# Two hyena projections on the un-normed input, scaled by 1/rms afterwards

## The chip, the cores and the metric

One core of a Trainium2 chip runs one launch of the kernel. The metric is the device time of that launch in microseconds (us). The kernel before takes 2434.83 us (median of 3 runs, 2433.78 to 2437.77).

## The reference, cut to what matters

The model is an encoder of four layers on one sequence of 512 tokens with 1024 channels, all in float32. Each layer adds a mixer and then a SwiGLU feed-forward block (2816 wide) to x. The mixers are hyena, window attention, pooling, hyena. Only the two hyena mixers (layers 0 and 3) are touched.

```
def rmsnorm(x, g):
    y = x * rsqrt(mean(x * x, axis=-1, keepdims=True) + EPS)
    return y * g

def hyena_mixer(xn, ...):                  # xn = rmsnorm(x, norm_mix[i])
    p = xn @ w_in + b_in                   # 1024 -> 3 * 1024
    pp = pad(p, one token on either side)
    p = conv_b + sum(pp[:, j:j + L] * conv_w[j] for j in range(3))
    x1, x2, v = split(p, 3, axis=-1)
    kf = rfft(hyena_filters(L, ...))       # an MLP with sine units on positions, independent of x
    z = v
    for o, gate in enumerate((x1, x2)):
        z = gate * (long_conv(z, kf[:, o]) + fbias[o] * z)
    return z @ w_out + b_out
```

The norm divides every token's channels by one number, so the product of the un-normed x * g with `w_in`, scaled by 1/rms of each token, is the same sum. The bias `b_in` comes after that scale.

## The kernel before

x stands channel by token: 8 tiles of 128 channels by 512 tokens. Every float32 value that goes into a matmul is split into a rounded part and a rest (`hi`, `lo` of weights; `ghs`, `gls` of the normed input), and a product is three passes on TensorE: hi with hi, lo with hi, hi with lo (`mm3`, L206 to L208). A weight tile (512 KB, `raw`) is loaded on SyncE's queue, cast on ScalarE (`hi`, L191) and its rest taken on VectorE (`lo`, L192), 4 times 2 instructions of 128x512 for each pair of tiles.

A hyena mixer cuts each of the three projections (part 0 and 1 the gates, part 2 the value v) into four groups of 256 channels. A job (part, group) is 2 output tiles x 8 input tiles x 3 passes = 48 passes of 128x512. Its sums stand in two `mm` banks of PSUM. `in_proj` reads them with three ScalarE activations (which add the bias and the padding, L604 to L606), runs a 3-tap convolution (one activation L609 and two VectorE instructions L611), and turns the result on TensorE (L629). The groups' long convolutions follow (`conv_in` L657, `conv_out` L703 and L706), then the output projection, whose sums VectorE adds into x (L724).

Ahead of the first projection stands the norm: squares on ScalarE (L224), their sum over tiles on VectorE (`ssq`, L225), a matmul with a matrix of means (L228), a small chain for the reciprocal root (L234 to L240), a matmul that spreads it over partitions (L254), a copy (`rstd`, L257). Then for each of the 8 tiles VectorE writes xn = x * g * rstd (tile `sq`, L514), ScalarE casts it (`ghs`, L515), VectorE takes the rest (`gls`, L516). `gx_split` (L260) is the feed-forward's version without rstd: `ghs` straight from x on ScalarE (L263), `gls` by one VectorE instruction (L264); the feed-forward then scales the finished sums with rstd (L293, L296).

In mixer 0 the filter's MLP is worked on at the same time: three matmuls with a sine chain of 7 VectorE instructions behind each (L331 to L337), the last of which gives `hh` (L360); then the filter matmuls of `hh` with `w3h` and `w3l` (L386, L387; VectorE writes `w3l`, L380). In mixer 3 most of that is ready by then.

Each engine takes its instructions in a fixed order, which is set when the program is built: each instruction has a priority from its place in the program and from the `high_priority` offset around it. `FRONT` and `BACK` list at which point of the program which job is written. Loads go out on SyncE in their own order, and 8 of them can be under way.

Of the kernel before, what the change touches and what calls it, by code (L numbers as in the profile page):

```python
# [12 lines left out]
AF = mybir.ActivationFunctionType  # L13
ALU = mybir.AluOpType
# [17 lines left out]
GS = 256  # L32
# [8 lines left out]
UB = 8  # L41
JOBS = [(0, 0), (0, 1), (1, 0), (0, 2), (1, 1), (0, 3), (1, 2), (1, 3)]
BACK = [[[], [(2, 2)], [(0, 2)], [(0, 3)], [(2, 3), (1, 2)], [], [(1, 3)], []],
        [[(2, 0), (2, 1), (0, 0), (0, 1)], [(2, 2)], [(1, 0), (0, 2)], [(2, 3)], [(1, 1), (0, 3)], [(1, 2)], [(1, 3)], []]]
WIDE = [[(0, 1), (0, 3), (1, 0), (1, 1)], [(1, 0), (1, 3)]]
CP = 5000
FP = 6000
AHEAD = 3000
FRONT = [[(2, 0)], [(2, 1)], [], [], [(0, 0)], [(0, 1)], [(1, 0)], [(1, 1)]]
XP = 13000  # L50
PI = math.pi
PI_DOWN = 3.1415925
# [58 lines left out]
class Kernel:  # L111
# [43 lines left out]
    def load_x(self):  # L155
        nc, t = self.nc, self.t
        vec = self.tl(self.per, [P, t["vec"].shape[1]], "vec")
        with self.tc.high_priority(offset=20000):
            nc.sync.dma_start(vec, t["vec"])
            for k in range(KD):  # L160
                nc.sync.dma_start(self.x[k], t["x"][:, k])
        at = {}
        o = 0
        for name, w in VEC:
            at[name] = vec[:, o:o + w]
            o += w
        col = lambda name, j: at[name][:, j:j + 1]
        self.g_mix = lambda i, k: col("norm_mix", KD * i + k)
        self.g_ffn = lambda i, k: col("norm_ffn", KD * i + k)
        self.pl_b, self.pl_s = at["pl_b"], at["pl_scale"]  # L170
        self.hy_bo = lambda i, k: col("hy_b_out", KD * i + k)
        self.hy_bi = lambda i, a, b: at["hy_b_in"][:, 24 * i + a:24 * i + b]
        self.hy_cb = lambda i, a, b: at["hy_conv_b"][:, 24 * i + a:24 * i + b]
        self.hy_cw = lambda i, a, b: at["hy_conv_w"][:, 72 * i:72 * i + 72].rearrange("p (j c) -> p j c", j=3)[:, :, a:b]
        self.hy_f = lambda i: at["hy_f"][:, 4 * i:4 * i + 4]
        self.gq, self.gk, self.sink = at["at_q_gain"], at["at_k_gain"], at["at_sink"]
        nc.scalar.mul(self.gq, self.gq, HD ** -0.5)


    def wload(self, w, k0, nk, c0, ncols):  # L180

        nc = self.nc
        with self.tc.high_priority(offset=10000):
            raw = self.tl(self.wp, [P, nk, ncols], "raw", bufs=WB[0])
            nc.sync.dma_start(raw, w[k0 * P:(k0 + nk) * P, c0:c0 + ncols].rearrange("(k p) c -> p k c", p=P))
            parts = []
            step = min(nk, 512 // ncols)
            for k in range(0, nk, step):
                hi = self.tl(self.wp, [P, step, ncols], "hi", F32R, bufs=WB[1])
                lo = self.tl(self.wp, [P, step, ncols], "lo", F32R, bufs=WB[1])  # L190
# [300 lines left out]
    def hyena(self, s, i):  # L491
        nc, t = self.nc, self.t
        with self.tc.tile_pool(name=f"hy{s}", bufs=2) as hp, self.tc.tile_pool(name=f"hc{s}", bufs=1) as h1:
            self.fwd = self.tl(h1, [P, 2, R, P], "fwd")
            self.u = {}
            steps = None
            with ExitStack() as front:
                if s in self.rn:
                    nc.sync.dma_start(self.fwd, t["dft_fwd"])
                else:  # L500
                    fp = front.enter_context(self.tc.tile_pool(name=f"fil{s}", bufs=2))
                    f1 = front.enter_context(self.tc.tile_pool(name=f"mlp{s}", bufs=1))
                    with self.tc.high_priority(offset=FP + 10000):
                        for _ in self.filter_features(f1, fp, self.aux, s):
                            pass
                    neg = self.tl(fp, [P, 2, P], "neg", bufs=1)
                    steps = self.filters(s, fp, self.fwd, neg, FP)
                    for _ in range(2):
                        next(steps)
                with self.tc.high_priority(offset=18000):  # L510
                    rstd = self.rstd_row(nc.vector)
                    for k in range(KD):
                        xn = self.tl(self.wk, [P, L], "sq")
                        nc.vector.scalar_tensor_tensor(xn, self.x[k], self.g_mix(i, k), rstd, op0=ALU.mult, op1=ALU.mult)  # L514
# [54 lines left out]
    def in_proj(self, hp, s, g, part):  # L569

        nc, t = self.nc, self.t
        n = GS // P
        u = self.tl(hp, [P, R, GS] if part != 1 else [P, n, L], "u", bufs=UB)
        ps = [self.tl(self.mm, [P, L], "mm") for _ in range(n)]
        c0 = part * D + g * GS
        for k0 in (0, 4):
            ws = self.wload(t["hy_w_in"][s], k0, 4, c0, GS)
            for k in range(4):  # L580
                for e in range(n):
                    c = slice(e * P, (e + 1) * P)
                    self.mm3(ps[e], ws[k][0][:, c], ws[k][1][:, c], self.gh[k0 + k], self.gl[k0 + k],
                             k0 + k == 0, k0 + k == KD - 1)
        self.flush()
        j0 = c0 // P
        cw = self.hy_cw(s, j0, j0 + n)
        cb = self.hy_cb(s, j0, j0 + n)
        if part < 2:
            rn = self.rn[s][g][:, part]  # L590
            cw0, cb0 = cw, cb
            cw = self.tl(hp, [P, 3, n], "cw", bufs=4)
            cb = self.tl(hp, [P, n], "cb", bufs=4)
            nc.vector.tensor_tensor(cw, cw0, rn.unsqueeze(1).broadcast_to([P, 3, n]), op=ALU.mult)
            nc.vector.tensor_tensor(cb, cb0, rn, op=ALU.mult)
        taps = []
        with self.tc.high_priority(offset=7000):
            for e in range(n):
                p = self.tl(hp, [P, L + 2 * P], "p")
                last = (R - 1) * P  # L600
                bias = self.hy_bi(s, j0 + e, j0 + e + 1)
                nc.gpsimd.memset(p[:, 0:1], 0.0)
                nc.gpsimd.memset(p[:, L + 2 * P - 1:], 0.0)
                nc.scalar.activation(p[:, P:L + P], ps[e], AF.Identity, bias=bias)  # L604
                nc.scalar.activation(p[:, 1:P], ps[e][:, last:L - 1], AF.Identity, bias=bias)
                nc.scalar.activation(p[:, L + P:L + 2 * P - 1], ps[e][:, 1:P], AF.Identity, bias=bias)  # L606
                a = u[:, e] if part == 1 else self.tl(hp, [P, L], "a")
                w = lambda q: cw[:, q, e:e + 1]
                nc.scalar.activation(a, p[:, P:L + P], AF.Identity, scale=w(1), bias=cb[:, e:e + 1])  # L609
                for q in (0, 2):  # L610
                    nc.vector.scalar_tensor_tensor(a, p[:, q * P:q * P + L], w(q), a, op0=ALU.mult, op1=ALU.add)  # L611
                taps.append(a)
        if part == 1:
            return u
        self.pending = u, taps
        return u
# [461 lines left out]
```

## Time and profile before

| what | value |
|---|---|
| median of 3 runs | 2434.83 us (2433.78 to 2437.77) |
| the profiled execution | 2435.6 us, of it a span of 2433.8 us |
| TensorE (PE) busy | 2366.2 us, 97% of the span |
| VectorE (DVE) busy | 1471.9 us, 60% |
| ScalarE (ACT) busy | 965.3 us, 40% |
| granted TensorE clock, mean | 0.989 |

The span runs from the first instruction to the last of the profiled execution; 1.8 us lie around it. Busy time is counted by engine, so shares over the span are means over stages with different limits. A clock of 1.00 is 2.4 GHz.

### The profile page before, as it was taken

The page shows a single profiled execution, that of the slowest core. Times are in us where ns is not written, and L with a number is a line of the kernel's source. Part 1 is how long each engine was busy: PE and PEld are TensorE (multiplying, and loading weights), DVE is VectorE, ACT ScalarE, POOL GpSimd, SP SyncE. Part 2 cuts the span into 40 slices and gives each one's busy share as a digit, 9 for nine tenths or more (in the row PEclk, how much of TensorE's full clock was granted, in tenths as well). Part 3 has the DMA queues.
Part 4 walks back from the last instruction along what each step waited for, and adds up shares of the span by engine and source line. Part 5 has one row for each costly group of instructions (what it writes and reads, how often), then busy time and mean ns, then how long its engine had stood idle before and what let it go on. Part 6 is the DMA issues. An engine that isn't in the chain of part 4 may idle for free.

```text
span 2433.8 us, 29324 instructions
## 1 busy us (share of the span) xinstructions
PE 2366.2 (97%) x10966; PEld 1951.8 (80%) x10966; DVE 1471.9 (60%) x2479; ACT 965.3 (40%) x1771; POOL 66.7 (3%) x178
## 2 busy tenths in 40 slices
PE   7999989999999899999999989999989999999999
PEld 5778878878887777888888878888878888888887
DVE  7989896464335798554443365444348998544432
ACT  5543325333234667443332363333235443433321
POOL 0210000000001021000000000000000000000000
PEclk9999999999999899999999989999999999999999
DMA  5342223433334132233333223333333222333332
GB/s 154 122 173 87 95 67 97 111 95 96 95 96 117 57 110 84 87 96 96 95 98 100 84 86 95 96 98 101 95 123 103 93 91 77 95 96 98 101 103 88
DMA packets 176834, 240.43 MB, mean 99 GB/s; under 512 B 8097, under 2 KB 137137, under 8 KB 174516
## 3 DMA queue, kind: packets, MB, share of 16 engines
q1 hardware_dynamic: 174852, 234.27, 31.2%
q0 software_dynamic: 1840, 4.29, 1.0%
q8 instruction: 86, 1.41, 0.2%
q14 instruction: 56, 0.46, 0.1%
HBM read 218.51 MB, written 20.02 MB: 98 GB/s over the span
## 4 chain that ended last, share of the span: by engine, by line
PE 93%; DVE 3%; ACT 2%; issue 1%; DMA 0%; SPq 0%; ACTq 0%; DVEq 0%
PE mm L206 16%; PE mm L207 16%; PE mm L208 16%; PE aux L208 10%; PE aux L207 10%; PE aux L206 10%; PE aux L428 2%; PE aux L706 2%; PE aux L703 1%; PE aux L657 1%; PE mm L919 1%; PE aux L648 1%; PE aux L649 1%; PE aux L438 1%; PE mm L906 1%
## 5 line engine op out<-in xcount | busy, mean ns | idle before, releaser
L192 DVE TENSOR_TENSOR lo<-raw,hi 128x512 fp32r<-128x512 f32 x700 | 483.9, 692 | 697.7 <-ACT hi L191 693.6
L191 ACT CAST hi<-raw 128x512 fp32r<-128x512 f32 x700 | 434.8, 622 | 1025.5 <-PE mm L207 653.8
L206 PE MATMUL mm<-ghs,hi 128*128 128x512 f32 x1168 | 460.7, 397 | 4.2 <-ACT ghs L515 4.2
L208 PE MATMUL mm<-ghs,lo 128*128 128x512 f32 x1168 | 459.6, 394 | 0.0
L207 PE MATMUL mm<-gls,hi 128*128 128x512 f32 x1104 | 435.6, 395 | 0.0
L208 PE MATMUL aux<-ghs,lo 128*128 128x512 f32 x704 | 274.3, 390 | 1.1 <-DVE lo L192 1.1
L206 PE MATMUL aux<-ghs,hi 128*128 128x512 f32 x704 | 274.3, 390 | 0.0
L207 PE MATMUL aux<-gls,hi 128*128 128x512 f32 x704 | 273.9, 389 | 0.0
L206 PEld LDWEIGHTS mm<-ghs,hi 128*128 128x128 f32 x1168 | 220.6, 189 | 55.5 <-ACT ghs L515 4.8
L208 PEld LDWEIGHTS mm<-ghs,lo 128*128 128x128 f32 x1168 | 220.1, 188 | 45.5 <-issue 0.4
L207 PEld LDWEIGHTS mm<-gls,hi 128*128 128x128 f32 x1104 | 208.1, 189 | 44.6 <-issue 2.1
L208 PEld LDWEIGHTS aux<-ghs,lo 128*128 128x128 f32 x704 | 132.2, 188 | 30.1 <-DVE lo L192 2.9
L207 PEld LDWEIGHTS aux<-gls,hi 128*128 128x128 f32 x704 | 132.2, 188 | 27.4
L206 PEld LDWEIGHTS aux<-ghs,hi 128*128 128x128 f32 x704 | 132.2, 188 | 27.1
L206 PE MATMUL mm<-hh,hi 128*128 128x512 f32 x352 | 137.0, 389 | 0.0
L208 PE MATMUL aux<-hh,lo 128*128 128x512 f32 x352 | 137.0, 389 | 0.0
L207 PE MATMUL mm<-hl,hi 128*128 128x512 f32 x352 | 137.0, 389 | 0.0
L206 PE MATMUL aux<-hh,hi 128*128 128x512 f32 x352 | 136.9, 389 | 0.0
L208 PE MATMUL mm<-hh,lo 128*128 128x512 f32 x352 | 136.9, 389 | 0.0
L207 PE MATMUL aux<-hl,hi 128*128 128x512 f32 x352 | 136.9, 389 | 0.0
L300 ACT CAST hh<-t 128x512 fp32r<-128x512 f32 x88 | 54.6, 620 | 109.6 <-DVE t L297 109.6
L296 DVE TENSOR_TENSOR t<-aux,rstd 128x512 f32<-128x512 f32 x88 | 60.5, 687 | 61.9 <-PE aux L208 61.9
(271 smaller groups left out, 3451.7 us busy)
## 6 DMA issues: line engine op xcount, KB each, us to landing
raw<-in_ff_w_gate SPq DMA_DIRECT2D x88, 512.0 KB
raw<-in_ff_w_up SPq DMA_DIRECT2D x88, 512.0 KB
raw<-in_ff_w_down SPq DMA_DIRECT2D x88, 512.0 KB
raw<-in_hy_w_in SPq DMA_DIRECT2D x48, 512.0 KB
kd<-k SPq DMA_DIRECT2D x32, 512.0 KB
kt<-kd SPq DMA_DIRECT2D x16, 1024.0 KB
raw<-in_hy_w_out SPq DMA_DIRECT2D x16, 512.0 KB
raw<-in_at_w_qkv SPq DMA_DIRECT2D x12, 512.0 KB
```

The source lines that it names most:

```text
L191: nc.scalar.copy(hi, raw[:, k:k + step])
L192: nc.vector.tensor_tensor(lo, raw[:, k:k + step], hi.bitcast(F32), op=ALU.subtract)
L206: mm(ps, ah, bh, start=first, stop=False)
L207: mm(ps, ah, bl, start=False, stop=False)
L208: mm(ps, al, bh, start=False, stop=last)
L296: nc.vector.tensor_tensor(t2, u[e], rstd, op=ALU.mult)
L300: nc.scalar.copy(a, t2)
L428: nc.tensor.matmul(po[:, ty, e], w, ab[:, r, e], start=m == 0, stop=m == 1)
L438: nc.tensor.matmul(pe[:, j, e], fwd[:, e, 2 * j], ab[:, 2 * j, e], start=True, stop=True)
L648: mm(ps[:, j, e], fwd[:, e, j], u[:, j], start=e == 0, stop=False)
L649: mm(ps[:, j, e], f2(e, j), u[:, 2 + j], start=False, stop=e == 1)
L706: mm(y[:, e, r * P:(r + 1) * P], v[:, e * P:(e + 1) * P], w, start=st, stop=sp)
```

## The change

`RAW = [(2, 0), (2, 1)]`: the first two value jobs run on the un-normed split. In each hyena mixer `gx_split` now writes `ghs` and `gls` without rstd, then `in_sums` writes the passes of the two jobs (one job's sums in two `mm` banks, the other's in one `aux` tile of two banks), then the norm's chain is written, and `short_conv` multiplies each of the four finished sums with rstd on VectorE (new tile `sq`) before the activations read it. After that the 8 triples xn, `ghs`, `gls` are written as before, over the same tiles, for the other ten jobs (priority 17000 in place of 18000). In `load_x` the first job's two weight tiles go out behind x tile 0 and behind x tile 3. In changed code line numbers are 1 to 26 higher than before: L206 to L208 become L210 to L212, L228 L232, L254 L258, L354 L358, L360 L364, L386 L390, L514 L524, L516 L526, L611 L637, L629 L655, L657 L683.

```
-FRONT = [[(2, 0)], [(2, 1)], [], [], [(0, 0)], [(0, 1)], [(1, 0)], [(1, 1)]]
+RAW = [(2, 0), (2, 1)]
+FRONT = [[], [], [], [], [(0, 0)], [(0, 1)], [(1, 0)], [(1, 1)]]
...
             for k in range(KD):
                 nc.sync.dma_start(self.x[k], t["x"][:, k])
+                if k in (0, 3):
+                    self.first.append(self.wload(t["hy_w_in"][0], 4 * len(self.first), 4, 2 * D, GS, 0))
...
+                with self.tc.high_priority(offset=18000):
+                    self.gx_split(lambda k: self.g_mix(i, k))
+                sums = [self.in_sums(s, g, part, room) for (part, g), room in zip(RAW, (self.mm, self.aux))]
+                with self.tc.high_priority(offset=18000):
+                    rstd = self.rstd_row(nc.vector)
...
-                with self.tc.high_priority(offset=18000):
-                    rstd = self.rstd_row(nc.vector)
+                for (part, g), ps in zip(RAW, sums):
+                    self.u[part, g] = self.short_conv(hp, s, g, part, ps, rstd)
+                with self.tc.high_priority(offset=17000):
                     for k in range(KD):
                         xn = self.tl(self.wk, [P, L], "sq")
                         nc.vector.scalar_tensor_tensor(xn, self.x[k], self.g_mix(i, k), rstd, op0=ALU.mult, op1=ALU.mult)
...
+    def in_sums(self, s, g, part, room=None):
+
         n = GS // P
-        u = self.tl(hp, [P, R, GS] if part != 1 else [P, n, L], "u", bufs=UB)
-        ps = [self.tl(self.mm, [P, L], "mm") for _ in range(n)]
-        c0 = part * D + g * GS
+        if room is self.aux:
+            both = self.tl(room, [P, n, L], "aux")
+            ps = [both[:, e] for e in range(n)]
+        else:
+            ps = [self.tl(self.mm, [P, L], "mm") for _ in range(n)]
...
+                src = ps[e]
+                if row is not None:
+                    src = self.tl(self.wk, [P, L], "sq")
+                    nc.vector.tensor_tensor(src, ps[e], row, op=ALU.mult)
...
-                nc.scalar.activation(p[:, P:L + P], ps[e], AF.Identity, bias=bias)
+                nc.scalar.activation(p[:, P:L + P], src, AF.Identity, bias=bias)
```

Three places in the engines' orders matter for the prediction. The first is the start of TensorE's row. Before, the filter's first features and the norm come ahead of the first projection pass:

```order
L354 MATMUL aux_123<-zf_119,fw_120 64x512
L228 MATMUL mm_235<-mean_10_81,ssq_212 128x1 x4
L254 MATMUL mm_251<-ident_87,rs_r_242 128x128 x4
L206 MATMUL mm_291<-ghs_85,hi_295 128x512
L206 MATMUL mm_292<-ghs_85,hi_295 128x512
```

Now the passes of job (2, 0) come first, and the norm's matmuls (L232, L258) stand 47 and 63 rows further on, in the midst of jobs (2, 0) and (2, 1):

```order
L210 MATMUL mm_149<-ghs_85,hi_100 128x512
L211 MATMUL mm_149<-gls_86,hi_100 128x512
L212 MATMUL mm_149<-ghs_85,lo_101 128x512
L210 MATMUL mm_150<-ghs_85,hi_100 128x512
L211 MATMUL mm_150<-gls_86,hi_100 128x512
```

The second place is where TensorE reaches the filter matmuls in mixer 0 (L386 to L387 before, L390 to L391 now). Before, job (0, 0), whose sums are `mm_773` and `mm_774`, has 12 of its 48 passes ahead of them, and the other 36 behind. In the changed kernel the last pass of job (2, 1) (row 101), the third filter features L358 (row 102) and a turn L655 stand ahead, and the first pass of job (0, 0), here `mm_795`, comes behind all eight of them:

```order
L655 MATMUL mm_439<-ident_87,a_422 128x128 x4
L390 MATMUL aux_389<-w3h_385,hh_363 128x512
L390 MATMUL aux_395<-w3h_385,hh_363 128x512
L655 MATMUL mm_445<-ident_87,a_434 128x128 x4
L391 MATMUL aux_395<-w3l_371,hh_363 128x512
L390 MATMUL aux_395<-w3h_385,hh_363 128x512
L391 MATMUL aux_395<-w3l_371,hh_363 128x512
L391 MATMUL aux_389<-w3l_371,hh_363 128x512
L390 MATMUL aux_389<-w3h_385,hh_363 128x512
L391 MATMUL aux_389<-w3l_371,hh_363 128x512
L210 MATMUL mm_795<-ghs_85,hi_799 128x512
```

So between the end of job (2, 1) and the first pass of job (0, 0) TensorE has only rows that wait for `hh` and `w3l`. The third place is VectorE's row ahead of `hh` in mixer 0 of the changed kernel. Before, the 16 instructions of the norm (L514, L516) lie 31 to 50 rows ahead of `hh`; now they stand among the third sine chain (L335 to L341) and the taps (L637):

```order
L524 SCALAR_TENSOR_TENSOR sq_491<-x_5_76,vec_95,rstd_312 128x512
L524 SCALAR_TENSOR_TENSOR sq_495<-x_6_77,vec_95,rstd_312 128x512
L341 TENSOR_SCALAR sa_352<-sa_352 128x512
L526 TENSOR_TENSOR gls_86<-sq_491,ghs_85 128x512
L526 TENSOR_TENSOR gls_86<-sq_495,ghs_85 128x512
L524 SCALAR_TENSOR_TENSOR sq_499<-x_7_78,vec_95,rstd_312 128x512
L524 SCALAR_TENSOR_TENSOR sq_503<-x_8_79,vec_95,rstd_312 128x512
L364 TENSOR_TENSOR hh_363<-sh_361,hh_363 64x512
L526 TENSOR_TENSOR gls_86<-sq_499,ghs_85 128x512
L526 TENSOR_TENSOR gls_86<-sq_503,ghs_85 128x512
L637 SCALAR_TENSOR_TENSOR a_434<-p_426,vec_95,a_434 128x512
L384 TENSOR_TENSOR w3l_371<-w3s_382,w3h_385 64x512
```

14 of the 16 are ahead of `hh`, and `w3l` stands 4 rows behind it; before, `w3l` (L380) stood ahead of `hh`. From VectorE's row 199 and TensorE's row 347 on, some 128 us into the run, both orders are the old ones up to mixer 3, where the same exchange is made: the two RAW jobs come straight behind the feed-forward's last pass, ahead of the norm's two matmuls.

## Rows read from the trace of the kernel before

**Rows 1.** The page's head: span, busy us (share of the span) and instructions.

```profile
span 2433.8 us, 29324 instructions
...
PE 2366.2 (97%) x10966; PEld 1951.8 (80%) x10966; DVE 1471.9 (60%) x2479; ACT 965.3 (40%) x1771; POOL 66.7 (3%) x178
```

**Rows 2.** Windows, mixer 0: length; busy PE, PEld, DVE, ACT, POOL; clock, DMA, GB/s.

```profile
0.00:23.10 23.10, 5.78 (x18) 3.84 (x18) 12.13 (x26) 10.82 (x19) 1.53 (x14) 1.00 0.80 254
23.10:40.00 16.90, 16.88 (x64) 12.90 (x65) 15.54 (x27) 10.38 (x19) 0.00 (x0) 1.00 0.23 63
40.00:60.00 20.00, 19.87 (x92) 15.33 (x91) 19.00 (x33) 13.31 (x27) 0.89 (x8) 1.00 0.41 123
60.00:80.00 20.00, 19.02 (x86) 15.03 (x85) 19.16 (x30) 12.43 (x19) 5.37 (x6) 1.00 0.34 109
```

**Rows 3.** ACT's timeline, 0 to 24: start, duration, line; idle before.

```profile
4.50 0.63 ACT L221 ACTIVATE ssq<-x 128x512 f32<-128x512 f32 x1 [1.16 <-DMA x<-in_x]
...
13.24 1.14 ACT L191 CAST hi<-raw 128x512 fp32r<-128x512 f32 x2 [1.10 <-DMA raw<-in_hy_w_in]
```

**Rows 4.** PE's timeline, 19 to 30.

```profile
18.96 2.05 PE L254 MATMUL mm<-ident,rs_r 128*128 128x128 f32 x8 [3.28 <-DVE rs_r L240]
23.12 2.07 PE L206 MATMUL mm<-ghs,hi 128*128 128x512 f32 x4 [2.11 <-ACT ghs L515]
```

**Rows 5.** DVE's timeline around hh.

```profile
52.38 0.69 DVE L360 TENSOR_TENSOR hh<-sh,hh 64x512 fp32r<-64x512 f32 x1
53.45 0.75 DVE L611 SCALAR_TENSOR_TENSOR a<-p,vec,a 128x512 f32<-128x512 f32 x1 [0.38 <-ACT a L609]
54.12 0.68 DVE L192 TENSOR_TENSOR lo<-raw,hi 128x512 fp32r<-128x512 f32 x1
54.72 0.74 DVE L611 SCALAR_TENSOR_TENSOR a<-p,vec,a 128x512 f32<-128x512 f32 x1
```

**Rows 6.** PE's timeline where projections resume.

```profile
55.08 0.39 PE L206 MATMUL mm<-ghs,hi 128*128 128x512 f32 x1
```

**Rows 7.** PE's waits, 0 to 140 us.

```profile
PE aux L386 <- DVE k L445: 2.2, 3, 1.0
```

**Rows 8.** DVE's groups over the span: busy, mean ns; idle before, releaser.

```profile
L296 DVE TENSOR_TENSOR t<-aux,rstd 128x512 f32<-128x512 f32 x88 | 60.5, 687 | 61.9 <-PE aux L208 61.9
...
L514 DVE SCALAR_TENSOR_TENSOR sq<-x,vec,rstd 128x512 f32<-128x512 f32 x16 | 11.3, 743 | 3.7 <-ACT rstd L257 3.7
```

**Rows 9.** Busy time by window, end of mixer 0.

```profile
260.00:280.00 20.00, 20.00 (x100) 16.67 (x99) 13.90 (x18) 7.64 (x15) 0.27 (x4) 1.00 0.31 106
...
320.00:340.00 20.00, 13.52 (x62) 10.88 (x61) 19.91 (x30) 1.86 (x3) 0.00 (x0) 0.85 0.16 52
```

**Rows 10.** PE's timeline, end of mixer 0.

```profile
335.47 0.80 PE L206 MATMUL mm<-zh,hi 128*128 128x512 f32 x1 [6.48 <-DVE x L724]
```

**Rows 11.** Busy time by window, front of mixer 3.

```profile
1800.00:1820.00 20.00, 12.81 (x48) 10.53 (x49) 14.58 (x35) 8.60 (x19) 0.21 (x4) 0.74 0.55 206
1820.00:1840.00 20.00, 19.89 (x91) 15.99 (x91) 11.38 (x16) 10.37 (x20) 0.27 (x4) 1.00 0.28 84
1840.00:1860.00 20.00, 20.00 (x94) 16.38 (x93) 19.98 (x29) 11.98 (x24) 0.27 (x4) 1.00 0.32 105
```

**Rows 12.** PE's timeline, front of mixer 3.

```profile
1799.33 0.39 PE L207 MATMUL mm<-hl,hi 128*128 128x512 f32 x1
1799.55 0.39 PE L208 MATMUL mm<-hh,lo 128*128 128x512 f32 x1
1803.57 1.05 PE L228 MATMUL mm<-mean,ssq 128*128 128x1 f32 x8 [3.63 <-DVE ssq L225]
1806.13 2.07 PE L254 MATMUL mm<-ident,rs_r 128*128 128x128 f32 x8 [1.50 <-DVE rs_r L240]
1810.31 2.07 PE L206 MATMUL mm<-ghs,hi 128*128 128x512 f32 x4 [2.11 <-ACT ghs L515]
...
1815.17 0.44 PE L206 MATMUL mm<-ghs,hi 128*128 128x512 f32 x1
```

More of the change, by code (lines that the diff above doesn't have):

```diff
@@ L43 @@
 BACK = [[[], [(2, 2)], [(0, 2)], [(0, 3)], [(2, 3), (1, 2)], [], [(1, 3)], []],
-        [[(2, 0), (2, 1), (0, 0), (0, 1)], [(2, 2)], [(1, 0), (0, 2)], [(2, 3)], [(1, 1), (0, 3)], [(1, 2)], [(1, 3)], []]]
+        [[(0, 0), (0, 1)], [(2, 2)], [(1, 0), (0, 2)], [(2, 3)], [(1, 1), (0, 3)], [(1, 2)], [(1, 3)], []]]
 WIDE = [[(0, 1), (0, 3), (1, 0), (1, 1)], [(1, 0), (1, 3)]]
@@ L159, in load_x @@
             nc.sync.dma_start(vec, t["vec"])
+            self.first = []
             for k in range(KD):
                 nc.sync.dma_start(self.x[k], t["x"][:, k])
+                if k in (0, 3):
+                    self.first.append(self.wload(t["hy_w_in"][0], 4 * len(self.first), 4, 2 * D, GS, 0))
         at = {}
@@ L177, in load_x, with wload @@
         nc.scalar.mul(self.gq, self.gq, HD ** -0.5)
-    def wload(self, w, k0, nk, c0, ncols):
+    def wload(self, w, k0, nk, c0, ncols, ahead=10000):
         nc = self.nc
-        with self.tc.high_priority(offset=10000):
+        with self.tc.high_priority(offset=ahead):
             raw = self.tl(self.wp, [P, nk, ncols], "raw", bufs=WB[0])
@@ L569, in in_proj @@
     def in_proj(self, hp, s, g, part):
-        nc, t = self.nc, self.t
+        return self.short_conv(hp, s, g, part, self.in_sums(s, g, part))
+    def in_sums(self, s, g, part, room=None):
         n = GS // P
-        u = self.tl(hp, [P, R, GS] if part != 1 else [P, n, L], "u", bufs=UB)
-        ps = [self.tl(self.mm, [P, L], "mm") for _ in range(n)]
-        c0 = part * D + g * GS
+        if room is self.aux:
[3 more added lines that the diff above has]
+            ps = [self.tl(self.mm, [P, L], "mm") for _ in range(n)]
         for k0 in (0, 4):
-            ws = self.wload(t["hy_w_in"][s], k0, 4, c0, GS)
+            ws = self.first.pop(0) if self.first else self.wload(self.t["hy_w_in"][s], k0, 4, part * D + g * GS, GS)
             for k in range(4):
@@ L584, in in_proj, with short_conv @@
                              k0 + k == 0, k0 + k == KD - 1)
+        return ps
+    def short_conv(self, hp, s, g, part, ps, row=None):
+        nc = self.nc
+        n = GS // P
+        u = self.tl(hp, [P, R, GS] if part != 1 else [P, n, L], "u", bufs=UB)
         self.flush()
-        j0 = c0 // P
+        j0 = (part * D + g * GS) // P
         cw = self.hy_cw(s, j0, j0 + n)
@@ L601, in in_proj @@
                 bias = self.hy_bi(s, j0 + e, j0 + e + 1)
+                src = ps[e]
+                if row is not None:
+                    src = self.tl(self.wk, [P, L], "sq")
+                    nc.vector.tensor_tensor(src, ps[e], row, op=ALU.mult)
                 nc.gpsimd.memset(p[:, 0:1], 0.0)
                 nc.gpsimd.memset(p[:, L + 2 * P - 1:], 0.0)
-                nc.scalar.activation(p[:, P:L + P], ps[e], AF.Identity, bias=bias)
-                nc.scalar.activation(p[:, 1:P], ps[e][:, last:L - 1], AF.Identity, bias=bias)
-                nc.scalar.activation(p[:, L + P:L + 2 * P - 1], ps[e][:, 1:P], AF.Identity, bias=bias)
+                nc.scalar.activation(p[:, P:L + P], src, AF.Identity, bias=bias)
+                nc.scalar.activation(p[:, 1:P], src[:, last:L - 1], AF.Identity, bias=bias)
+                nc.scalar.activation(p[:, L + P:L + 2 * P - 1], src[:, 1:P], AF.Identity, bias=bias)
                 a = u[:, e] if part == 1 else self.tl(hp, [P, L], "a")
```

## The prediction

> **What bounds the kernel now.** The page's head first: TensorE is busy for 97% of a span of 2433.8 us [rows 1]. Where it is never idle, a saving on another engine is worth nothing, so I looked for the places where it waits or where VectorE is just as full.
>
> At the start nothing is multiplied for the projections before 23.12 us [rows 4]. The first x tile is there at 4.50, the first weights at 13.24 [rows 3]. What ends last is the norm's chain: TensorE stands idle for 3.28 us ahead of L254 and for 2.11 us ahead of the first pass [rows 4]. This is the stop that the change goes for.
>
> Behind it the picture turns. In the windows from 23.1 to 80 us VectorE is busy for 15.54 of 16.90, 19.00 of 20 and 19.16 of 20 us, TensorE for 16.88, 19.87 and 19.02 [rows 2]. Both are full. Up to 140 us TensorE's own waits there are 2.2 us in three pieces, on VectorE's filter work [rows 7]. At 260 to 280 us TensorE is full and VectorE has 6.1 us free; at 320 to 340 VectorE is full (19.91) and TensorE stands for 6.48 us, until VectorE's L724 frees a sum [rows 9, 10]. So an engine that runs late in mixer 0's front has little to catch up with: TensorE's slack up to 260 us is hardly more than those 2.2 us, and what VectorE gets done late near the mixer's end goes straight into the end.
>
> Mixer 3 begins with the same chain, behind a TensorE that was running: idle 3.63, 1.50 and 2.11 us [rows 12], 7.2 in all, and a granted clock of 0.74 in that window [rows 11]. The first 11 passes take from 1810.31 to 1815.17, 0.44 us each, where the feed-forward's passes follow at 0.22 [rows 12]: 2.4 us more. VectorE is idle for 5.4 and 8.6 us in the two windows from 1800 to 1840, and from 1840 both engines are full (20.00 and 19.98) [rows 11].
>
> **The change part by part.** Added are, in each mixer, 8 casts on ScalarE, 8 L264-like instructions on VectorE, and 4 scalings of a sum. A scaling is L296's kind (687 ns), the other costs what L514 costs (743 ns) [rows 8]. Back to back the start-to-start pitch is shorter: a three-operand instruction of 0.75 us is followed after 0.67, one of 0.68 after 0.60 [rows 5]. So 8 x 0.67 + 4 x 0.61 = 7.8 us of VectorE per mixer. ScalarE is busy for 13.31 of 20 us at most in the front [rows 2], so its casts are hidden. No pass and no load is added.
>
> *Mixer 0, the start.* From x tile 0 (4.50) to the first weights (13.24) some 2.4 MB come in (7 x tiles, the filter's inputs, one weight tile), 280 bytes per ns. A weight tile then takes 1.9 us: the first is there at about 6.4, its cast and rest at about 7.8, and x tile 7 at about 15 in place of 11.5. The first pass begins at about 8, 15 us earlier than 23.12. The passes then follow VectorE, which has 8 `gls`, 4 weight rests and 7 `ssq` sums, 12 us of work, from 5 us on with waits for x. `ssq` is ready at about 20. The norm's matmuls stand inside TensorE's row of jobs (2, 0) and (2, 1), so nothing else waits for them long; from the mean matmul to `rstd` I take 5.5 to 7 us (in mixer 3 it is 6.7 to the first pass, with xn and its cast in it [rows 12]), so `rstd` at about 26.5. Both jobs, 96 passes, are through at about 36 us, the third filter features at about 39. So far TensorE is some 25 passes ahead of before.
>
> *Mixer 0, the new stop.* Now the order decides. Behind the third features all that TensorE has are the turns and the filter matmuls, which want `hh`. VectorE's queue from `rstd` to `hh` holds 43 instructions: 4 scalings, 14 of the second norm, two sine chains and the rest of the first, 5 taps, weights. With 0.67 for the three-operand ones, 0.60 for the others and 0.33 to 0.42 for the half-size or single-operand ones this is 25 us; from about 27.2 that makes 52, and it waits some 2 us for the third features, since they stand behind the last pass of job (2, 1). `hh` is done at about 54.4. Before, it was done at 52.38 + 0.69 = 53.1 [rows 5], 1.3 us earlier. So TensorE, which has nothing else from about 40, stands until 54.4, 14 us: the 15 us gained at the start are given back in one piece. Then `w3l` is late: two `gls` and a tap are ahead of it (2.5 us, so at about 57), and the eight filter matmuls end at about 59. Job (0, 0) begins at about 59.2. Before, it went on at 55.08 [rows 6] with 12 of its passes done (2.7 us). TensorE is thus 59.2 - 55.1 + 2.7 = 6.8 us late. VectorE is 1.3 us late at `hh` and has 1.8 us more behind it that was done earlier before (2 `gls` and a tap against a weight rest that is left out): 3.2.
>
> Of TensorE's 6.8 the 2.2 us of waits [rows 7] can vanish, since what is waited for is only 3.2 late: 4.6 remain. If VectorE sets the pace, 3.2 remain, and if nothing is made up, 6.8. I take +4 us, near the row of waits.
>
> *Mixer 3.* The RAW jobs follow the feed-forward's last pass without a stop, at full rate: 7.2 + 2.4 us are saved on TensorE at first. But 96 passes and two input transforms take TensorE only to about 1828, and the normed `ghs` for job (0, 0) wants the four scalings and the second norm behind them on VectorE, at about 1832: 4 us of stop. At the end of job (0, 0) TensorE is some 3.3 us ahead of before. VectorE's 7.8 us more fill the idle time of 5.4 and 8.6 us between 1800 and 1840 [rows 11]; its last `gls` comes out about 0.2 us ahead of the old order. From there VectorE is full, TensorE's transforms wait for it, and 3.3 us of lead on an engine that waits for the other are worth nothing. I take 0, with -3.3 (VectorE not the limit) and +3 (second norm later than I count) as ends.
>
> The clock in the new stops: behind the 7.2 us of stops of mixer 3 it is 0.74 in the window, behind the 6.48 us at 335 it is 0.85 [rows 9, 11], so a slow start behind 14 us is counted in (about 2 us, in the 59 above), behind 4 us it is not. The Trainium skill ("TensorE: Matmul & The Clock Gate", section "HAM oscillation — how this bites in real kernels") says that TensorE falls back to its lower clock in waits between groups of matmuls and begins the next group there. By that rule mixer 3's new stop would cost up to those 2.4 us again, and TensorE's lead would be 0.9 in place of 3.3; the sum stays, since VectorE is taken as the limit either way. The trace agrees with the rule at the two stops named, and shows none of 4 us in a piece.
>
> *The sum.* +4 and 0. The profiled execution took 2435.6 us (span 2433.8 and 1.8 around it), 0.8 over the median of 2434.83; the same sum on the median gives 2439.
>
> **Rivals.** *The head start stays* (faster). If TensorE keeps its lead, because VectorE reaches `hh` early (by 45 us, not 54), mixer 0 gains up to 11, and mixer 3 up to its 9.6. For it: the stops removed are real rows. Against it: VectorE is 95% busy behind 23 us [rows 2] and gets 7.8 us more ahead of `hh`. It decides from `hh` before 48 on. About 2415. *Mixer 0 comes out even, mixer 3 keeps TensorE's lead.* VectorE's 3 us are absorbed in the 6.1 us that it has free at 260 to 280 [rows 9], and TensorE makes up its lag, since more than the 2.2 us is slack; mixer 3 keeps 3 to 5. About 2431. *The stop in mixer 0 costs more* (slower, the other side of my near-nothing). Each us that `hh` or `w3l` comes later moves TensorE by as much; with nothing made up and `hh` 2 us later it is +9, about 2444. It counts as slower from `hh` at 55.3 on. *The change doesn't do what it says*, the loads in particular: if the first weights come no earlier than 12 us, passes begin at 13 and still end before `hh`; the sum is the same, so this needs no price.
>
> **How the numbers follow.** A measurement of this kernel tells 0.2%, 4.9 us, from no change: 2430.0 to 2439.7. Chances: my forecast (2436.5 to 2442) 0.45, the stop costs more 0.20, even with a lead in mixer 3 0.22, the head start stays 0.13. The forecast's own range straddles the bound, about half on each side. Slower: 0.20 + 0.21 = 0.41. Faster: 0.13 and a third of the even case, 0.20. Same: 0.39. The range leaves out about one in ten on each side: 2424 to 2446.
>
> **What would show it.** First pass at about 8 us, 96 passes done by 36 to 40, then a TensorE stop of about 14 us that ends with `hh` at 54.4; filter matmuls at half rate; job (0, 0) at 59; mixer 0's last L724 about 4 us later than before. In mixer 3 no stop at 1800, one of about 4 us ahead of the first pass of job (0, 0), and the windows from 1840 both full. Wrong would make it: `hh` well before 50, a stop under 8 us, or a TensorE that has its lead still at 100 us.

## The result, and the profile after

The changed kernel takes 2452.9 us (median of 4 runs, 2452.59 to 2452.98), the kernel before beside it 2436.3 us (4 runs). The ratio is 1.0071, with a 95% interval of 1.006 to 1.0083: 16.6 us slower. The forecast was 2439 us with a range up to 2446.

The page's head of the changed kernel's profiled execution, to set against [rows 1]:

```profile
span 2451.2 us, 29359 instructions
...
PE 2372.7 (97%) x10966; PEld 1953.7 (80%) x10966; DVE 1486.1 (61%) x2503; ACT 975.3 (40%) x1787; POOL 65.4 (3%) x178
```

The span is 17.4 us longer, TensorE's busy time only 6.5. So most of the loss is time in which TensorE stands, and the rest is passes that took longer.

Where it comes from is read best from the ends of the stages. VectorE's L724 (now L750) adds a mixer's output to x. Its last instruction in mixer 0 and in mixer 3, first before, then in the changed kernel (VectorE's timeline: start, duration, instruction):

```profile
353.88 0.74 DVE L724 SCALAR_TENSOR_TENSOR x<-mm,vec,x 128x512 f32<-128x512 f32 x1
```

```profile
2047.76 0.74 DVE L724 SCALAR_TENSOR_TENSOR x<-mm,vec,x 128x512 f32<-128x512 f32 x1
```

```profile
365.07 0.75 DVE L750 SCALAR_TENSOR_TENSOR x<-mm,vec,x 128x512 f32<-128x512 f32 x1
```

```profile
2065.14 0.74 DVE L750 SCALAR_TENSOR_TENSOR x<-mm,vec,x 128x512 f32<-128x512 f32 x1
```

Mixer 0 ends 11.2 us later, mixer 3 17.4. Behind mixer 3 nothing more is lost. Between the two mixers, where the program is unchanged, the distance grows too: the first attention window, before and in the changed kernel 11.2 us later, has TensorE at a mean clock of 0.91 and of 0.83 (same columns as [rows 2]):

```profile
740.00:760.00 20.00, 17.12 (x72) 13.51 (x71) 12.99 (x22) 11.41 (x15) 8.14 (x14) 0.91 0.65 172
```

```profile
751.20:771.20 20.00, 16.99 (x64) 13.43 (x63) 12.42 (x21) 11.16 (x15) 8.16 (x14) 0.83 0.62 172
```

There and in the scores behind it 2.5 us are lost (the same rows run 11.2 us later ahead of it and 13.7 behind it), so mixer 3 itself costs 3.7. The feed-forward's last pass ahead of mixer 3, at 1799.55 before [rows 12], now stands here:

```profile
1813.22 0.39 PE L212 MATMUL mm<-hh,lo 128*128 128x512 f32 x1
```

That the change costs these 2.5 us is not shown. The stretch from mixer 0's last add to that pass holds the same program in every kernel here; the twenty profiled executions took between 1441.7 and 1448.2 us for it, 1445.7 before and 1448.2 in the changed kernel. A mixer's own length, counted inside one execution, is steadier, as the experiments show.

Mixer 0's front in TensorE's timeline:

```profile
8.30 0.80 PE L210 MATMUL mm<-ghs,hi 128*128 128x512 f32 x1 [8.30 <-ACT hi L195]
...
36.45 0.39 PE L212 MATMUL aux<-ghs,lo 128*128 128x512 f32 x1
39.82 1.70 PE L358 MATMUL aux<-sh,fw 64*128 64x512 f32 x2 [2.98 <-DVE a L637]
41.45 0.90 PE L655 MATMUL mm<-ident,a 128*128 128x128 f32 x3
```

```profile
56.90 1.22 PE L390 MATMUL aux<-w3h,hh 128*128 128x512 f32 x2 [14.34 <-DVE hh L364]
...
62.43 0.63 PE L210 MATMUL mm<-ghs,hi 128*128 128x512 f32 x1
62.86 0.63 PE L211 MATMUL mm<-gls,hi 128*128 128x512 f32 x1
...
64.81 0.40 PE L211 MATMUL mm<-gls,hi 128*128 128x512 f32 x1
65.04 0.39 PE L212 MATMUL mm<-ghs,lo 128*128 128x512 f32 x1
```

The first pass runs at 8.30, the last of the RAW jobs at 36.45, the third filter features at 39.82, and then TensorE stands for 14.34 us until `hh`. Job (0, 0) begins at 62.43, with 0.43 us from pass to pass, and from 64.81 on with 0.23. VectorE's timeline around `hh`:

```profile
42.28 0.74 DVE L524 SCALAR_TENSOR_TENSOR sq<-x,vec,rstd 128x512 f32<-128x512 f32 x1
...
56.16 0.69 DVE L364 TENSOR_TENSOR hh<-sh,hh 64x512 fp32r<-64x512 f32 x1
```

The second norm's first xn (L524) starts at 42.28, although `rstd` is copied by 27.8, and `hh` is written at 56.16. What the stop costs beside its length stands in the windows (against [rows 2] and [rows 9]):

```profile
0.00:23.10 23.10, 14.80 (x58) 11.66 (x59) 14.82 (x26) 15.45 (x28) 1.52 (x14) 1.00 0.77 239
...
40.00:60.00 20.00, 4.80 (x13) 2.38 (x13) 18.75 (x32) 9.68 (x18) 0.32 (x6) 0.51 0.00 0
60.00:80.00 20.00, 18.63 (x81) 14.87 (x80) 15.39 (x26) 9.80 (x13) 4.82 (x6) 0.90 0.30 93
```

TensorE is busy for 14.80 us in the first 23.1 (5.78 before) and for 4.80 in the stretch from 40 to 60 (19.87 before). The mean clock is 0.51 there and 0.90 from 60 to 80. From there on TensorE makes nothing up. Its waits up to 140 us hold new ones (us in total, times, longest):

```profile
PE aux L390 <- DVE hh L364: 14.3, 1, 14.3
...
PE aux L415 <- POOL mx L406: 1.4, 1, 1.4
PE aux L390 <- DVE ab L392: 1.1, 1, 1.1
...
PE aux L442 <- DVE ab L441: 0.6, 1, 0.6
```

In mixer 3 the stop at the layer's start is gone and the clock stays at 1.00 there (against [rows 11]):

```profile
1800.00:1820.00 20.00, 20.00 (x94) 16.52 (x92) 11.61 (x18) 8.62 (x15) 0.21 (x4) 1.00 0.44 153
1820.00:1840.00 20.00, 19.83 (x97) 16.18 (x97) 10.20 (x28) 11.39 (x24) 0.27 (x4) 1.00 0.49 165
1840.00:1860.00 20.00, 15.88 (x57) 11.65 (x56) 18.68 (x29) 11.35 (x21) 0.13 (x2) 0.83 0.17 52
```

But VectorE, which has less than 12 of 20 us of work in the first two windows, starts the second norm only here:

```profile
1842.36 0.69 DVE L627 TENSOR_TENSOR sq<-aux,rstd 128x512 f32<-128x512 f32 x1
...
1844.77 0.75 DVE L524 SCALAR_TENSOR_TENSOR sq<-x,vec,rstd 128x512 f32<-128x512 f32 x1
```

The scaling of job (2, 1)'s first sum (L627) comes at 1842.36, the first xn at 1844.77, and TensorE waits for its cast:

```profile
1846.33 1.22 PE L210 MATMUL mm<-ghs,hi 128*128 128x512 f32 x2 [4.01 <-ACT ghs L525]
```

Behind these 4.01 us its clock is low once more (0.83 in the window from 1840). Near the mixer's end TensorE waits for VectorE to free a sum, first before, then in the changed kernel:

```profile
2028.34 0.50 PE L206 MATMUL mm<-zh,hi 128*128 128x512 f32 x1 [0.73 <-DVE x L724]
```

```profile
2044.08 0.79 PE L210 MATMUL mm<-zh,hi 128*128 128x512 f32 x1 [4.67 <-DVE x L750]
```

Counted from the feed-forward's last pass, the pass ahead of this wait still starts 1.9 us earlier than before (225.8 us behind it, 227.7 before), and the pass behind the wait 2.1 us later (230.9 and 228.8).

### The profile page after: what moved, and what is told of

The parts are those of the page before. It is cut to its first block, busy times and chain, and to the rows that moved or that the text cites. A ratio compares the mean times of both kernels' runs of the same rounds, so it can differ in the third digit from the quotient of the medians.

```text
span 2451.2 us, 29359 instructions
## 1 busy us (share of the span) xinstructions
PE 2372.7 (97%) x10966; PEld 1953.7 (80%) x10966; DVE 1486.1 (61%) x2503; ACT 975.3 (40%) x1787; POOL 65.4 (3%) x178
## 3 DMA queue, kind: packets, MB, share of 16 engines
q0 software_dynamic: 1840, 4.29, 0.9%
## 4 chain that ended last, share of the span: by engine, by line
PE 92%; DVE 4%; ACT 2%; issue 1%; DMA 0%; POOL 0%; SPq 0%; ACTq 0%; DVEq 0%; POOLq 0%
PE mm L210 16%; PE mm L211 16%; PE mm L212 16%; PE aux L212 10%; PE aux L211 10%; PE aux L210 10%; PE aux L432 2%; PE aux L732 2%; PE aux L683 1%; PE aux L729 1%; PE mm L945 1%; PE aux L674 1%; PE aux L675 1%; PE aux L442 1%; PE mm L655 1%
## 5 line engine op out<-in xcount | busy, mean ns | idle before, releaser
L210 PE MATMUL mm<-ghs,hi 128*128 128x512 f32 x1136 | 449.1, 397 | 12.3 <-ACT hi L195 8.3
L212 PE MATMUL mm<-ghs,lo 128*128 128x512 f32 x1136 | 448.0, 394 | 0.0
L211 PE MATMUL mm<-gls,hi 128*128 128x512 f32 x1072 | 425.1, 397 | 0.2
L212 PE MATMUL aux<-ghs,lo 128*128 128x512 f32 x736 | 286.9, 390 | 1.1 <-DVE lo L196 1.1
L210 PE MATMUL aux<-ghs,hi 128*128 128x512 f32 x736 | 287.2, 390 | 0.0
L211 PE MATMUL aux<-gls,hi 128*128 128x512 f32 x736 | 286.8, 390 | 0.0
L210 PEld LDWEIGHTS mm<-ghs,hi 128*128 128x128 f32 x1136 | 214.8, 189 | 61.6 <-ACT hi L195 11.5
L212 PEld LDWEIGHTS mm<-ghs,lo 128*128 128x128 f32 x1136 | 214.6, 189 | 44.3 <-issue 0.4
L212 PEld LDWEIGHTS aux<-ghs,lo 128*128 128x128 f32 x736 | 138.2, 188 | 31.4 <-DVE lo L196 2.9
L211 PEld LDWEIGHTS aux<-gls,hi 128*128 128x128 f32 x736 | 138.2, 188 | 30.1 <-issue 1.6
L210 PEld LDWEIGHTS aux<-ghs,hi 128*128 128x128 f32 x736 | 138.2, 188 | 28.3
L210 PE MATMUL mm<-hh,hi 128*128 128x512 f32 x352 | 137.0, 389 | 0.0
L212 PE MATMUL aux<-hh,lo 128*128 128x512 f32 x352 | 137.0, 389 | 0.0
L210 PE MATMUL aux<-hh,hi 128*128 128x512 f32 x352 | 136.9, 389 | 0.0
L212 PE MATMUL mm<-hh,lo 128*128 128x512 f32 x352 | 136.9, 389 | 0.0
```

The costliest lines, as they stand in the source:

```text
L210: mm(ps, ah, bh, start=first, stop=False)
L211: mm(ps, ah, bl, start=False, stop=False)
L212: mm(ps, al, bh, start=False, stop=last)
```

## The experiments

Times are medians, each taken beside the kernel before on the same chip (2435 to 2437 us), and a gain or loss on before is the ratio's. By that the change itself costs 17.3 us. Two theories went in. A: TensorE's new stops, for `hh` in mixer 0 and for the second norm in mixer 3, and what follows from them, are the loss. B: VectorE's 7.8 us more in each mixer are it, wherever TensorE then stands.

**Which part costs what.** Each half of the change alone, the loads alone, and VectorE's added work alone. In the first two, a set `RAWS` says which mixer takes the new path, the other keeps the old one.

```
+RAWS = (0,)        # the other kernel: (1,), without the loads
...
-                sums = [self.in_sums(s, g, part, room) for (part, g), room in zip(RAW, (self.mm, self.aux))]
+                if s in RAWS:
+                    sums = [self.in_sums(s, g, part, room) for (part, g), room in zip(RAW, (self.mm, self.aux))]
```

Mixer 0 alone, with the loads. Expected:

> Changed kernel with the old norm-first order in mixer 3; mixer 0 and the loads as changed. Theory A (most of the loss is mixer 0's new 14 us stop of TensorE and the lag it leaves): mixer 0 ends 11 us later than before, the total is +11 to +14 us on before. Rival B (the loss is spread evenly, since each mixer has the same 7.8 us more on VectorE): about +8.

Measured: 2448.47 us, ratio 1.0047 [1.0032, 1.0062], +11.4. Mixer 3 alone. Expected:

> Before with the change in mixer 3 alone, loads as before. Theory A: no stop at the layer's start but 4 us of stop ahead of job (0, 0), mixer 3 ends 3 to 5 us later than before: total +3 to +5. Rival B: +8. Rival C (mixer 3's loss in the changed kernel only comes from its shifted clock phase): 0.

Measured: 2440.58 us, 1.0017 [1.0007, 1.0026], +4. The parts add up to 15.5 of the 17.3; the loss is not spread evenly, and mixer 3's is its own. The loads alone. Expected:

> Before, with only the two weight tiles loaded behind x tiles 0 and 3. Theory A: x tile 7 and with it the norm's chain come some 3.5 us later, the first pass at 25 to 27 us in place of 23.1; VectorE does the weights' rests earlier, so total 0 to +3.5. Rival (the early weights help): -2 to 0.

Measured: 2435.65 us, 0.9999 [0.999, 1.0009]: nothing, neither way. VectorE's work alone, in the kernel before:

```
+                    for k in range(12):
+                        xn = self.tl(self.wk, [P, L], "sq")
+                        nc.vector.tensor_tensor(xn, self.x[k % KD], rstd, op=ALU.mult)
```

> Before, with 12 more VectorE instructions of 128x512 (x times rstd into a scratch tile) behind the norm in each mixer, 7.3 us each, as many as the change adds; the output is untouched. Theory A (the order of the second norm and hh costs, the work alone little): mixer 0 +3 to +6, mixer 3 0 to +2, total +3 to +8. Rival B (the added VectorE work is the whole cost): +7 in each mixer, +14 in all.

Measured: 2442.72 us, 1.0023 [1.0013, 1.0032], +5.6. So as much VectorE work, with no new stop of TensorE over 2.1 us in mixer 0, costs a third of the change's loss. The work alone is not it. It is not evenly priced either: in the profiled execution (2445.3 us, the slowest of ten) mixer 0 ends 6.5 us later than before, and mixer 3 takes 1.7 us longer.

**Is it hh?** The stop in mixer 0 ends with `hh`, so the filter's MLP, which needs no x, was put first (ahead of the RAW jobs in the program, at priority 30000):

```
+                if s not in self.rn:
+                    with self.tc.high_priority(offset=FEATURES):
+                        for _ in self.filter_features(f1, fp, self.aux, s):
+                            pass
                 with self.tc.high_priority(offset=18000):
                     self.gx_split(lambda k: self.g_mix(i, k))
```

> The changed kernel with the filter's MLP (three matmuls, sine chains, hh) written and loaded ahead of the RAW jobs in mixer 0, so hh is done at about 35 us in place of 56.8. Theory A (mixer 0's loss is the stop of TensorE for hh and the restart behind it): the 14 us stop becomes one of some 5 us for the second norm, mixer 0 ends 3 to 6 us later than before in place of 11, total +8 to +11 on before in place of +16.6. Rival B (the second norm on VectorE sets the pace whoever waits for it): the stop only changes its name, total +15 to +17.

Measured: 2448.99 us, 1.005 [1.0032, 1.0068], +12 (runs from 2444 to 2450). The control, the MLP first in the kernel before:

> Control: before with the filter's MLP ahead of the x loads' work, as in the run with features first. Both theories: hh is not what mixer 0 waits for there, so -2 to +1.

Measured: 2437.82 us, 1.0003 [0.9993, 1.0012]. An early `hh` wins 5 us of 17.3, near what A had, and leaves 12. Mixer 0 ends at 359.51, 5.6 us later than before where it was 11.2; mixer 3's loss, which has nothing to do with `hh`, is in the 12 as well. So `hh` is where mixer 0's stop showed, and about half of its loss is left without it. Next, no second norm at all: every job runs on the un-normed split and each of the 24 sums is scaled.

```
-                with self.tc.high_priority(offset=17000):
-                    for k in range(KD):
...
+                self.row = rstd
...
-        return self.short_conv(hp, s, g, part, self.in_sums(s, g, part))
+        return self.short_conv(hp, s, g, part, self.in_sums(s, g, part), self.row)
```

> The changed kernel with no second norm: all 12 jobs of both mixers run on the un-normed split and all 24 sums are scaled on VectorE (16 instructions and 8 casts fewer, 20 scalings more: some 2 us more on VectorE than the change, 9.7 more than before). Theory A (stops for the second norm and for hh behind it are the loss): no stop at 1846, mixer 3 at 0 or some us ahead of before, mixer 0 +2 to +6, total 0 to +6. Rival B (VectorE work is the price): 2 us more per mixer than the change, total +20.

> The same without a second norm, and the filter's MLP first: neither hh nor a second norm is waited for. Theory A: -5 to +1 on before, and better than without the MLP first. Rival B: +19.

Measured: 2445.71 us, 1.004 [1.0026, 1.0054], and with the MLP first 2450.11 us, 1.0053 [1.0037, 1.0069]: +10 and +13. Neither theory had it. TensorE's waits in mixer 3 of the first of the two show why its gain was small:

```profile
PE mm L650 <- DVE a L632: 8.9, 2, 8.7
PE aux L724 <- DVE c L712: 8.1, 1, 8.1
```

No stop for a second norm, but 8.9 us for taps and 8.1 for the transforms' products, both VectorE's.

**The shared ring.** Why does xn start at 42 us with `rstd` there at 27.8, and at 1844.77 behind the scaling at 1842.36? xn and the scaled sums are both tiles `sq`, of which there are two buffers, handed out in the program's order: four scaled sums, then xn of tile 0. The third and fourth scaled sum belong to job (2, 1), so the second norm's first instruction stands behind the end of that job, whatever its priority. The changed kernel's trace fits this. ScalarE copies `rstd` at 27.22, and its last read of the third and of the fourth scaled sum (L632) is here:

```profile
27.22 0.59 ACT L261 COPY rstd<-mm 128x512 f32<-128x512 f32 x1 [0.22 <-PE mm L258]
...
40.72 0.38 ACT L632 ACTIVATE p<-sq,vec 128x127 f32<-128x127 f32 x1
...
48.62 0.38 ACT L632 ACTIVATE p<-sq,vec 128x127 f32<-128x127 f32 x1
```

The first xn starts at 42.28, behind the first of these reads. Until the second of them has ended, one buffer is left and xn come one by one; from then on they come in pairs:

```profile
45.59 0.74 DVE L524 SCALAR_TENSOR_TENSOR sq<-x,vec,rstd 128x512 f32<-128x512 f32 x1
...
48.72 1.41 DVE L524 SCALAR_TENSOR_TENSOR sq<-x,vec,rstd 128x512 f32<-128x512 f32 x2
```

In mixer 3 the third sum's last read ends at 1844.46, and xn starts at 1844.77. This can be tested with nothing else moved by hand: two buffers of their own for the scaled sums.

```
+                self.sc = front.enter_context(self.tc.tile_pool(name=f"sc{s}", bufs=2))
...
-                    src = self.tl(self.wk, [P, L], "sq")
+                    src = self.tl(self.sc, [P, L], "scaled")
```

> The changed kernel, but the scaled sums have two buffers of their own and no longer share the two of the tile sq with the second norm's xn. Theory A, second form (the second norm starts late because its first xn needs a buffer that the scaled sums of job (2, 1) hold till that job ends; the stop for it is the loss): xn starts at about 28 us in place of 42, job (0, 0) follows job (2, 1) without the 14 us stop, mixer 3's 4 us stop goes; a shorter stop for hh stays in mixer 0. Total 0 to +6 on before, some 12 below the changed kernel. Rival B (the added VectorE work is the price, 5.6 us as the run with more VectorE work has it, wherever the stops stand): +8 to +16.

Measured: 2435.10 us, 0.9992 [0.9983, 1.0001]: 2 us below before, which can't be told from no change, and some 18 below the changed kernel. VectorE's timeline of this run, the first xn (L525) and the first scaling (L628):

```profile
27.91 1.40 DVE L525 SCALAR_TENSOR_TENSOR sq<-x,vec,rstd 128x512 f32<-128x512 f32 x2
...
43.96 0.67 DVE L628 TENSOR_TENSOR scaled<-mm,rstd 128x512 f32<-128x512 f32 x1
```

xn starts at 27.91, 14 us sooner, now ahead of the scalings. With the buffers free the engines' orders, which are built from the program, come out otherwise too: 23 passes of job (0, 0) now stand ahead of the filter matmuls in TensorE's row, where the changed kernel had none:

```profile
53.12 0.77 PE L210 MATMUL mm<-ghs,hi 128*128 128x512 f32 x1
...
60.43 0.62 PE L390 MATMUL aux<-w3h,hh 128*128 128x512 f32 x2
```

So this run shows the ring together with the orders that follow from it. TensorE still stands, for the third filter features, whose sine chain is now behind the norm:

```profile
45.96 2.07 PE L358 MATMUL aux<-sh,fw 64*128 64x512 f32 x2 [9.33 <-ACT sh L343]
```

Mixer 3 alone and mixer 0 alone with own buffers:

> Before with the change in mixer 3 alone and the two buffers of their own for the scaled sums. Theory A, second form: no 4 us stop ahead of job (0, 0), mixer 3 2 to 6 us ahead of before, total -2 to -6, where mixer 3 alone with shared buffers gave +4. Rival B: +2 to +6.

> Mixer 0 alone changed, with the loads and with buffers of their own for the scaled sums. The run with both mixers was -2 and mixer 3 alone -3.3, so mixer 0 alone should be +1 (0 to +3), where with shared buffers it was +11.4: some 10 us of mixer 0's loss are the shared ring.

Measured: mixer 3 2434.26 us, 0.9987 [0.9977, 0.9996], and mixer 0 2437.13 us, 1.0006 [0.9997, 1.0015]. With shared buffers they were +4 and +11.4; so the ring, with the orders that follow from it, is 7.3 us in mixer 3 and 9.9 in mixer 0, together as much as the 17.3. The traces say the same of mixer 3 alone. From the feed-forward's last pass to the mixer's last add it takes 248.0 to 248.4 us in the six kernels that leave it as before, 251.9 to 252.9 in the three that have the change with shared buffers, and 245.0 to 245.2 in the four that have it with own ones.

**What the rest is.** The early start by 15 us still wins nothing. With own buffers the MLP was put first again, in both mixers' kernel and with mixer 0 alone:

> The same with the filter's MLP first in mixer 0: neither hh nor the second norm is late. Theory A, second form: no stop over 3 us before 60 us, mixer 0 ends 0 to 6 us ahead of before, total -6 to 0. Rival B: +4 to +12, with the waits further on, at transforms that want VectorE.

> Mixer 0 alone as in the run with own buffers and the MLP first, mixer 3 as before. Theory A, second form: -3 to 0. Rival B: +4 to +8.

Measured: 2440.01 us, 1.0011 [1.0002, 1.002], and 2444.47 us, 1.0029 [1.002, 1.0039]; 5 and 6 us worse than with the MLP where it was, so A's second form fails here too. TensorE now stands at a turn, for the taps:

```profile
53.59 1.08 PE L658 MATMUL mm<-ident,a 128*128 128x128 f32 x4 [12.30 <-DVE a L640]
```

So the stop moves from `hh` to the features to the taps (14.34, 9.33, 12.30 us): whichever of VectorE's chains is put last is the one that TensorE finds missing. Is it then TensorE's order, in which ready passes stand behind rows that wait? Job (0, 0) was given a high priority (16500), in both mixers and in mixer 3 alone, or the turns none:

```
+        if (part, g) in NEXT:
+            with self.tc.high_priority(offset=16500):
+                sums = self.in_sums(s, g, part)
```

> The changed kernel with two buffers of their own for the scaled sums, and job (0, 0) at a high priority, so that its passes stand behind the third filter features and two turns, ahead of the other turns and the filter matmuls, in both mixers. Theory A, second form (with the second norm early, what is left of the loss are stops at rows that stand ahead of work that is ready): -2 to -8 on before. Rival B (VectorE's 7.8 us per mixer are what is left, wherever TensorE waits): -2 to +3, as without the priority.

> Mixer 3 alone with buffers of their own, and job (0, 0) at the high priority there: the 6.1 us that TensorE waits for taps ahead of the turns should shrink. Theory A: -4 to -8. Rival B: -2 to -4, as without the priority.

> The same, but the turns of mixer 3 at no priority in place of job (0, 0) at a high one. Theory A: -4 to -8. Rival B: -2 to -4.

> Mixer 3 alone with buffers of their own once more, in more rounds, beside the two that it is compared with: -3 (-1 to -5).

Measured: 2458.75 us, 1.0093 [1.0077, 1.0108]; 2450.29 us, 1.0059 [1.0047, 1.0072]; 2442.09 us, 1.0022 [1.0012, 1.0031]; and the plain one 2433.32 us, 0.9987 [0.9978, 0.9996]. All three moves lose, and what either theory expected of them was missed. In the second the turns, which now stand behind some of job (0, 0), wait for their taps:

```profile
PE mm L665 <- DVE a L647: 17.7, 2, 10.2
```

The priority also moves the job's weight loads, casts and rests ahead of VectorE's taps, so these runs do not show the order by itself. Last, VectorE's work taken away: the second norm without its `gls` (the ten later jobs multiply the un-normed rest).

```
-                        nc.vector.tensor_tensor(self.gl[k], xn, self.gh[k].bitcast(F32), op=ALU.subtract)
```

> The changed kernel with buffers of their own for the scaled sums, and the second norm without its gls (8 VectorE instructions, 4.8 us, in each mixer; the ten later jobs multiply the un-normed rest in its place, so the output is off). If VectorE's added work is what eats the early start: 5 to 9 us below the run with own buffers, -7 to -11 on before. If it is the order of TensorE's rows: within 2 us of it, -4 to 0 on before.

Measured: 2421.07 us, 0.9941 [0.9927, 0.9955], 14.4 us below before and so 12.4 below the run with own buffers, for 9.6 us less work on VectorE: more than either side had. In mixer 3 TensorE's waits are all but gone (6.3 us in the run with own buffers):

```profile
PE aux L212 <- DVE lo L196: 0.3, 1, 0.3
PE mm L655 <- DVE a L637: 0.2, 1, 0.2
```

Part of that is that rows also stand in another order there: with less on VectorE the turns come earlier and job (0, 0) is woven between them. In mixer 0, where TensorE's row is nearly the one with own buffers, its end moved by 2 us only. Of the 14.0 us between the two profiled executions about 8 lie in mixer 3 (245.2 us, now 237.3), 2 in mixer 0 and 4 in the unchanged stretch between them, where one execution differs from another by as much.

## Why the prediction was wrong

**Right:** the start (first pass at 8.30, forecast 8), the RAW jobs' end (36.45, forecast 36), the stop for `hh` (14.34 us, forecast 14), no stop at 1800 and one of 4.01 us at 1846 (forecast 4; with the 13.7 us shift of the layer taken off at 1832.6, forecast 1832). The rival in which the head start stays was rightly thought unlikely, and that the stop costs more, the rival on the other side, is the case that came, beyond its price of 2444. One reading was off without weight in the sum: at 39 us TensorE was 39 passes ahead (96 against 57), where it says some 25.

**Wrong in mixer 0:** the step "Of TensorE's 6.8 the 2.2 us of waits [rows 7] can vanish", and so "I take +4 us". The lag was 10.0 by the same sum when job (0, 0) began (62.43 - 55.08 [rows 6] + 2.7). Of the 3.2 us more than counted 2.5 are `hh`'s, done at 56.85 in place of 54.4; the rest lies between `hh` and job (0, 0), 5.6 us in place of 4.8, where TensorE ran at half rate (a slow start of about 2 us was in the sum). And nothing was made up. In place of the 2.2 us of waits [rows 7] came others of 3.1 (1.4, 1.1 and 0.6), on VectorE and GpSimd. The lag at the end was 11.2, above even the upper end of that term, 6.8.

**Wrong in mixer 3:** the step "I take 0", and in it "VectorE's 7.8 us more fill the idle time of 5.4 and 8.6 us between 1800 and 1840". The stop and TensorE's lead were as counted, and the lead was worth nothing, as it says. But the idle time was not filled, since the second norm started only 31.6 us behind the feed-forward's last pass (1844.77). VectorE in the 40 us behind that pass, before and in the changed kernel (columns as in [rows 2]):

```profile
1799.55:1819.55 20.00, 12.76 (x48) 10.16 (x47) 14.58 (x35) 8.55 (x19) 0.21 (x4) 0.74 0.53 197
1819.55:1839.55 20.00, 19.89 (x91) 15.98 (x90) 11.38 (x16) 10.37 (x20) 0.27 (x4) 1.00 0.30 92
```

```profile
1813.22:1833.22 20.00, 19.83 (x98) 16.28 (x97) 15.13 (x37) 13.39 (x28) 0.34 (x6) 1.00 0.71 249
1833.22:1853.22 20.00, 15.99 (x61) 12.15 (x60) 13.59 (x21) 10.28 (x22) 0.27 (x4) 0.83 0.13 41
```

So VectorE was idle for 14.0 us there and is for 11.3 now (8.2 with own buffers). It comes to the add that TensorE waits for at the end 2.1 us later than before. The other 1.6 of the mixer's 3.7 us are slow passes behind that wait of 4.67 us: the clock is 0.83 in the 10 us from 2043.7, and it was 1.00 behind the 0.73 us before. The stop of 4.01 us had slow passes too (0.83 from 1840 to 1860), where the prediction left the clock alone, but they only took lead. The rule of the Trainium skill that the prediction cited ("TensorE: Matmul & The Clock Gate", section "HAM oscillation — how this bites in real kernels") is that matmuls begin at the lower clock behind a wait. The trace agrees with it at both waits, 4.01 and 4.67 us, with 0.43 us from pass to pass behind the first and 0.23 ahead of it. The mixer's 3.7 us lie a little above the upper end of +3.

**Not in the sum at all:** 2.5 us between the mixers, where the program is unchanged. They lie within what single executions differ by there (1441.7 to 1448.2 us), and they don't follow from the later start: the kernel with job (0, 0) at a high priority in both mixers ends mixer 0 at 364.90, as late as the changed one, and takes 1443.2 us for the stretch. The clock in the first attention window is 0.91 in seventeen of the twenty executions, and 0.83 to 0.85 in three whose mixer 0 ends 0.5, 6.5 and 11.2 us later than before. Why it falls differently is not settled.

**What the prediction read without seeing its reason:** that the second norm stands late in VectorE's row. The row was taken as it stood, and VectorE's 7.8 us as what mattered. The reason is a ring of two buffers shared by xn and the scaled sums, and the runs with own buffers show that it costs, with the orders that follow from it, 10 us in mixer 0 and 7 in mixer 3, as much as the whole loss. VectorE's work costs 5.6 by itself in the kernel before. That it is also what eats the early start once the ring is gone is not shown: taking 4.8 us of it out of each mixer brings 12, but 2 in mixer 0 and 8 in mixer 3, where the order changed with it. How much of this is the work and how much the order stays open. The kernel with mixer 3 alone changed and own buffers beats the kernel before by 3 us, in two sets of runs. Moving the second norm's `gls` to another engine was not tried.

## What to carry to other kernels

When a step is moved so that it should run early, look at the buffers that its first instruction needs as well as at priorities: a scratch tile whose ring is shared with something that waits for the old work's end ties the new order to it. An earlier start of the busiest engine is worth only what the next busiest can follow with; if the stretch behind is full on both, count the added work there and expect the stop to come back elsewhere. Price a new stop of TensorE with the slow passes behind it, and do not assume that a lag is made up where the trace shows both engines full.

## What the runs showed of the hardware

Means of the granted clock between 0.5 and 1.00 are stretches at its two levels, 1.2 and 2.4 GHz. The 20 us that hold the stop of 14.34 us, which ends at 56.90, have a mean TensorE clock of 0.51, and the 20 us behind them 0.90. In these it did the rest of the filter matmuls and its first passes, 0.43 us apart where they are 0.23 apart from 64.81 on. So the low rate did not end with the first row that it ran. With 4.01 us in a piece it was 0.83 over the 20 us around the stop, and behind 4.67 us it was 0.83 over the next 10. And a stretch of 1445 us of unchanged program took from 1441.7 to 1448.2 us in twenty executions, a spread as large as many of the effects measured here; its length did not follow its start.
